# Products 512 columns wide in a two-layer decoder trunk: two token halves side by side, gate and up token-major with transposes back

## The chip, the core and the metric

The kernel runs on one core of one Trainium2 chip. Its engines work side by side, each through its own queue in order: TensorE (PE; its loading of the stationary operand is shown apart, as PEld), VectorE (DVE), ScalarE (ACT), GpSimd (POOL) and SyncE (SP, whose queue issues the DMAs). The metric is the time of one execution in microseconds (us), the median of several runs.

## What is computed

Two layers on 256 tokens (S) of 1024 features (D), float32. Layer 0 mixes tokens by causal attention (8 heads of 128; with 256 tokens there is one block, so the selection of past blocks adds nothing), layer 1 by a gated convolution of width 3. Each is followed by a SwiGLU feed-forward with D_FF = 2816. Scale, shift and gate of every sub-layer come from a vector c.

```python
for i in range(DEPTH):
    mod = sc @ w_ada[i] + b_ada[i]                       # sc = silu(c)
    sh_m, sc_m, g_m, sh_f, sc_f, g_f = jnp.split(mod, 6, axis=-1)
    h = modulate(x, norm_mix[i], sh_m, sc_m)
    y = moba_attention(h, ...) if i % 2 == 0 else short_conv(h, ...)   # both end in a product with 1024 x 1024 weights
    x = x + g_m[:, None, :] * y
    h = modulate(x, norm_ffn[i], sh_f, sc_f)
    g, u = jnp.split(h @ w_gate_up[i], 2, axis=-1)
    x = x + g_f[:, None, :] * ((jax.nn.silu(g) * u) @ w_down[i])
```

## The kernel before

**Products.** Every float32 operand is split into a high and a low float32r part, and every product is three PE instructions (`mm3`, L285): high by high, high by low, low by high. The one that is loaded has 128 columns, the one that moves has 256 (258 in the raw products below). A chunk of weights, up to 1024 rows by 256 columns, arrives by one DMA of 1 MB (`load`, L82, into one of five buffers `wf`); ACT casts it to the high part `wh` (L98), DVE subtracts to get the low part `wl` (L99), each in two halves.

**Feature-major.** The residual stream `xT` holds features on the partitions and the 256 tokens along the free axis. In `feat_gemm` and `out_proj` the weights are loaded and the 256 tokens move; the operands are pairs of separate tiles (high, low): `ov` and `zv` (input of the output projections of layers 0 and 1), `a0` and `a1` (input of the down-projections), `f0` and `f1` (normed input of gate and up).

**Feed-forward** (`ffn`, L466). Gate and up are done in 11 chunks `j` of 256 features each. The first goes by `raw_gemm` (L437), which multiplies the residual before its norm is known and corrects by the norm afterwards; the other ten fill `pg` and `pu`, then silu on ACT, `a = s * pu` on DVE (L481), and the split of `a` into the pair `av` (L434, L435). The down-projection `out_proj` (L406) goes through four groups of two output tiles, each with three chunks of 8, 8 and 6 blocks of 128 rows.

**The chain of a norm.** When an output tile of a projection is done, `residual` (L404, DVE) adds it to `xT` straight from the accumulator (PSUM), and `Norm.take` (L357) squares it (ACT), sums (POOL, L364, L367), and makes the raw pair: high part on ACT (L373), low part on DVE (L374). After the fifth tile the shift's columns are appended (L380, L381). The first raw product of the next stage reads these columns, so PE waits for L381; its third group of products waits for the sums (`ms`, L387), its fifth for the row of norms (`rr`, L335). The output projections `op_o` and `op_co` go through the groups [0, 1], [2], [3] of two tiles each; `op_d` is the down-projection.

**What sets the order.** The stream of chunks is a fixed list; between the weights stand 56 chunks of the modulation (`wa`), which DVE multiplies and adds up (L116). `get` prepares two chunks ahead of the one that PE takes up. Within these bounds a scheduler sets each engine's order before the run, and each engine keeps it.

**End.** The last down-projection's tiles are added to `xT`, turned to token-major by PE (L828), copied by ACT (L832) and stored by five DMAs (`store`, L825).

Of the kernel before, what the change touches and what calls it, by code (L numbers as in the profile page):

```python
# [31 lines left out]
def trunk_kernel(ctx: ExitStack, tc: tile.TileContext, x, c, w_ada, b_ada, norm_mix, norm_ffn, w_qkv, w_o,  # L32
# [69 lines left out]
    mod = const.tile([P, DEPTH * 48], F32, name="mod")  # L102
    acc_of = {}
    late, gets = [], [0]

    def ada_piece(l, part, i):
# [131 lines left out]

    def ffn_chunks(l):
        gu, dn = [], []  # L240
        for j in range(KF // 2):
            gu.append(w(("g", l, j), w_gate_up[l][:, j * CW:][:, :CW]))
            gu.append(w(("u", l, j), w_gate_up[l][:, D_FF + j * CW:][:, :CW]))
# [47 lines left out]
    def feat_gemm(parts, xs, nk):  # L291
        xh, xl = xs
# [7 lines left out]
    def tok_gemm(parts, xs, nk, between={}):  # L300
        xh, xl = xs
# [49 lines left out]
    class Norm:  # L351
        """Sums of squares over the features, gathered as the residual's tiles come."""
# [4 lines left out]
        def take(self, k):  # L357
# [13 lines left out]
            rh, rl = self.raw  # L371
# [30 lines left out]

# [463 lines left out]
```

## Time and profile before

| | |
|---|---|
| median of 3 runs | 625.7 us (625.13 to 626.88) |
| span of the profiled execution, first to last instruction | 622.1 us |
| the median less this span | 3.6 us |
| granted TensorE clock, mean | 0.999 |
| busy: PE, PEld, DVE, ACT, POOL | 98%, 96%, 76%, 52%, 3% |
| bytes over the DMA queues | 156.07 MB, mean 251 GB/s |

The page gives no other time of the profiled execution than its span. A row of the timeline gives start and duration in us, engine, line, operation, what is written and read, shape and count, and in brackets the idle time before it with what ended it. PE's durations overlap, since a product's end is still draining when the next one starts: the time that a product takes from PE is the distance of two starts, its pitch. A row of the stages' table gives from:to, length, then for PE, PEld, DVE, ACT and POOL the busy time with the number of instructions, the granted clock, the DMA engines' busy share, and GB/s. A row of the groups gives line, engine, operation, names, shapes, count, busy time and mean duration in ns, and the engine's idle time before these instructions with its causes.

### The profile page before, as it was taken

What the parts mean: (1) busy time and instruction counts of PE and PEld (TensorE: products, weight loads), DVE (VectorE), ACT (ScalarE), POOL (GpSimd) and SP (SyncE); (2) the same over time, 40 slices, a digit from 0 to 9 for tenths busy, and PEclk for the clock granted to TensorE, in tenths of its full rate; (3) what the DMA queues carried; (4) which work ended last, traced back from release to release, by engine and by line L of the source; (5) the groups of instructions that cost most, each with busy time, mean ns of one, the idle gap of its engine ahead of it and who ended that gap; (6) DMA issues with size and microseconds to landing.
All of it is one profiled execution on the core that took longest, in us unless ns stands there. A gap on an engine that the chain in (4) does not pass through costs nothing.

```text
span 622.1 us, 12512 instructions
## 1 busy us (share of the span) xinstructions
PE 609.7 (98%) x5291; PEld 595.8 (96%) x5291; DVE 473.6 (76%) x668; ACT 323.1 (52%) x518; POOL 19.2 (3%) x26
## 2 busy tenths in 40 slices
PE   7999999999999999999999999999999999999997
PEld 5789999999999999999999999998999999999997
DVE  5567999989989899979888989658976467644440
ACT  5335977466655455535355745545744435533330
POOL 0000000020000000000110000012000000000000
PEclk9999999999999999999999999999999999999999
DMA  9999999966699999798998497646388677655200
GB/s 271 329 331 354 385 370 335 303 219 223 210 323 322 347 333 335 257 318 303 319 302 278 133 304 241 210 138 205 108 299 271 201 225 235 204 188 178 94 18 17
DMA packets 127455, 156.07 MB, mean 251 GB/s; under 512 B 2822, under 2 KB 114856, under 8 KB 127400
## 3 DMA queue, kind: packets, MB, share of 16 engines
q1 hardware_dynamic: 127400, 155.28, 75.6%
q8 instruction: 41, 0.67, 0.5%
q14 instruction: 14, 0.11, 0.1%
HBM read 154.22 MB, written 1.05 MB: 250 GB/s over the span
## 4 chain that ended last, share of the span: by engine, by line
PE 88%; DMA 3%; DVE 3%; issue 3%; ACT 1%; SPq 0%; POOLq 0%; POOL 0%; ACTq 0%
PE pu L289 7%; PE pu L288 7%; PE op_d L287 7%; PE pu L287 7%; PE op_d L289 7%; PE op_d L288 7%; PE pg L289 6%; PE pg L288 6%; PE pg L287 6%; DMA wa<-in_w_ada_dram 2%; DMA wf_qk<-in_w_qkv_dram 1%; PE pv L287 1%; PE pb L288 1%; PE pv L289 1%; PE pb L287 1%
## 5 line engine op out<-in xcount | busy, mean ns | idle before, releaser
L116 DVE SCALAR_TENSOR_TENSOR acc<-wa,sc,acc 128x1024 f32<-128x1024 f32 x70 | 89.8, 1283 | 8.8 <-DMA wa<-in_w_ada_dram 7.5
L98 ACT ACTIVATE wh_d<-wf_d 128x1024 fp32r<-128x1024 f32 (+1 forms) x48 | 45.5, 981 | 69.7 <-issue 47.2
L99 DVE TENSOR_TENSOR wl_d<-wf_d,wh_d 128x1024 fp32r<-128x1024 f32 (+1 forms) x48 | 53.6, 1144 | 30.7 <-ACT wh_d L98 30.5
L98 ACT ACTIVATE wh_u<-wf_u 128x1024 fp32r<-128x1024 f32 x44 | 44.3, 1051 | 45.3 <-issue 34.5
L98 ACT ACTIVATE wh_g<-wf_g 128x1024 fp32r<-128x1024 f32 x44 | 45.5, 1050 | 40.7 <-issue 40.7
L99 DVE TENSOR_TENSOR wl_u<-wf_u,wh_u 128x1024 fp32r<-128x1024 f32 x44 | 52.7, 1233 | 14.0 <-ACT wh_u L98 14.0
L99 DVE TENSOR_TENSOR wl_g<-wf_g,wh_g 128x1024 fp32r<-128x1024 f32 x44 | 54.5, 1245 | 2.1 <-ACT wh_g L98 2.0
L287 PE MATMUL op_d<-a1h,wh_d 128*128 128x256 f32 x176 | 50.3, 286 | 0.0
L287 PE MATMUL op_d<-a0h,wh_d 128*128 128x256 f32 x176 | 50.2, 285 | 0.0
L289 PE MATMUL op_d<-a1h,wl_d 128*128 128x256 f32 x176 | 50.0, 284 | 0.0
L289 PE MATMUL op_d<-a0h,wl_d 128*128 128x256 f32 x176 | 50.0, 284 | 0.0
L288 PE MATMUL op_d<-a1l,wh_d 128*128 128x256 f32 x176 | 49.6, 282 | 0.0
L288 PE MATMUL op_d<-a0l,wh_d 128*128 128x256 f32 x176 | 49.5, 281 | 0.0
L289 PE MATMUL pg<-f1h,wl_g 128*128 128x256 f32 x160 | 44.8, 280 | 0.0
L289 PE MATMUL pu<-f1h,wl_u 128*128 128x256 f32 x160 | 44.8, 280 | 0.0
L287 PE MATMUL pg<-f1h,wh_g 128*128 128x256 f32 x160 | 44.6, 279 | 0.0
L288 PE MATMUL pg<-f1l,wh_g 128*128 128x256 f32 x160 | 44.6, 279 | 0.0
L287 PE MATMUL pu<-f1h,wh_u 128*128 128x256 f32 x160 | 44.6, 279 | 0.0
L288 PE MATMUL pu<-f1l,wh_u 128*128 128x256 f32 x160 | 44.6, 279 | 0.0
L287 PE MATMUL pg<-f0h,wh_g 128*128 128x256 f32 x160 | 44.5, 278 | 0.0
L289 PE MATMUL pg<-f0h,wl_g 128*128 128x256 f32 x160 | 44.4, 278 | 0.0
L289 PE MATMUL pu<-f0h,wl_u 128*128 128x256 f32 x160 | 44.4, 278 | 0.0
(315 smaller groups left out, 2103.6 us busy)
## 6 DMA issues: line engine op xcount, KB each, us to landing
wa<-in_w_ada_dram SPq DMA_DIRECT2D x40, 1024.0 KB, 6.1
wf_g<-in_w_gate_up_dram SPq DMA_DIRECT2D x22, 1024.0 KB, 6.6
wf_u<-in_w_gate_up_dram SPq DMA_DIRECT2D x22, 1024.0 KB, 7.5
wf_d<-in_w_down_dram SPq DMA_DIRECT2D x16, 1024.0 KB, 6.3
wa<-in_w_ada_dram SPq DMA_DIRECT2D x16, 512.0 KB, 7.1
wf_d<-in_w_down_dram SPq DMA_DIRECT2D x8, 768.0 KB, 5.7
wf_qk<-in_w_qkv_dram SPq DMA_DIRECT2D x8, 512.0 KB, 8.1
wf_v<-in_w_qkv_dram SPq DMA_DIRECT2D x4, 1024.0 KB, 7.5
```

The costliest lines, as they stand in the source:

```text
L98: nc.scalar.activation(wh[:, a:b], wf[:, a:b], AF.Copy)
L99: nc.vector.tensor_sub(wl[:, a:b], wf[:, a:b], wh[:, a:b].bitcast(F32))
L116: nc.vector.scalar_tensor_tensor(acc, w[:, kk], sc[:, k:k + 1], acc, op0=ALU.mult, op1=ALU.add)
L287: nc.tensor.matmul(ps, ah, bh, start=first, stop=False, skip_group_check=True)
L288: nc.tensor.matmul(ps, ah, bl, start=False, stop=False, skip_group_check=True)
L289: nc.tensor.matmul(ps, al, bh, start=False, stop=last, skip_group_check=True)
```

## The change

1. **Pairs in one tile.** High and low part of an activation lie in one tile (`[P, 2, nk, S]`), so that both can move in one instruction.
2. **`mm512` in `out_proj`.** For `op_o`, `op_co` and the down-projection of layer 0, the weights' high part is loaded once and the activations' high and low part move as 512 columns; then the low part of the weights with the high part of the activations, 256 columns. Two instructions stand where there were three. The accumulator has two halves, and `residual` adds one after the other: two DVE instructions for each tile instead of one.
3. **Gate and up token-major.** After the raw chunk come 5 blocks of 512 features instead of 10 of 256. The activations are loaded (128 tokens at a time) and 512 columns of weights move (`tok_wide`). A weight chunk is 512 rows by 512 columns, again 1 MB. Silu and product make `a` token-major, and `to_pair` turns it back: 8 PE transposes for each block, placed after the second k-step of the next gate block, and the split reads their PSUM tile.
4. **Last down-projection token-major** (`project`), 512 output features moving, in two halves of 6 chunks; `store` multiplies by the gate, adds the residual and stores, in four DMAs. The residual is turned to token-major earlier, between products of gate and up (`to_tokens`), the gate is made as a row on all partitions (`gate_rows`: two float32 products of 512 columns, and a DMA of the bias), and the sum over partitions in three bfloat16 parts goes for this one modulation.

Core of the diff (the pairs' indexing, comments and moved tiles left out):

```diff
+    def ps_wide(name):
+        return psum.tile([P, 2 * CW], F32, tag="gemm", name=name, bufs=4)
...
+        if (l, part) == (DEPTH - 1, G_F):
+            late.append((gets[0], lambda: gate_rows(acc)))
+            return
...
+    def gate_rows(acc):
+        for n in range(2):
+            cs = slice(n * 2 * CW, (n + 1) * 2 * CW)
+            ps = ps_misc(f"gate_ps_{n}")
+            nc.tensor.matmul(ps, one.to_broadcast([P, P]), acc[:, cs], start=True, stop=True)
+            nc.vector.tensor_add(last["gate"][:, cs], last["gate"][:, cs], ps)
...
+    WIDE = 2 * CW
+    GU_BLOCKS = (D_FF - CW) // WIDE
+    DOWN = ((0, 4), (4, 4), (8, 4), (12, 4), (16, 4), (20, 2))
...
+    def mm512(ps, lhs, both, first, last):
+        ah, al = lhs
+        nc.tensor.matmul(ps, ah, both, start=first, stop=False, skip_group_check=True)
+        nc.tensor.matmul(ps[:, 1], al, both[:, 0], start=False, stop=last, skip_group_check=True)
+
     def residual(ps, l, gate, k):
-        nc.vector.scalar_tensor_tensor(xT[:, k], ps, mcol(l, gate, k), xT[:, k], op0=ALU.mult, op1=ALU.add)
+        for n in range(2):
+            nc.vector.scalar_tensor_tensor(xT[:, k], ps[:, n], mcol(l, gate, k), xT[:, k], op0=ALU.mult, op1=ALU.add)
...
-                    mm3(pss[j, o], (wh[:, k, cs], wl[:, k, cs]), (xs[0][:, base + k], xs[1][:, base + k]),
-                        base + k == 0, base + k == total - 1)
+                    mm512(pss[j, o], (wh[:, k, cs], wl[:, k, cs]), xs[:, :, base + k],
+                          base + k == 0, base + k == total - 1)
...
+    def to_pair(pair, k, rows):
+        pt = ps_alt(f"ft_{k}")
+        for o in range(2):
+            for t in range(2):
+                nc.tensor.transpose(pt[:, o * S + t * P:][:, :P], rows[t][:, o * P:(o + 1) * P], ident)
+        split(pair, slice(k, k + 2), pt.rearrange("p (o s) -> p o s", s=S))
+
+    def tok_wide(pss, keys, xs, between={}, final=False):
+        total, base = sum(nk for _, nk in keys), 0
+        for i, (key, nk) in enumerate(keys):
+            wh, wl = get(key)
+            steps = [(k, t) for k in range(nk) for t in range(2)]
+            if final and i == len(keys) - 1:
+                steps.sort(key=lambda s: s[1])
...
+                mm3(pss[t], (xs[:, 0, base + k, ts], xs[:, 1, base + k, ts]), (wh[:, k], wl[:, k]),
+                    base + k == 0, base + k == total - 1)
+            base += nk
...
+    def store(j, t, cs, ps):
+        y = tmp.tile([P, WIDE], F32, tag="s", name=f"y_{j}_{t}")
+        nc.vector.tensor_mul(y, ps, last["gate"][:, cs])
+        nc.vector.tensor_add(y, y, last["x"][:, t, cs])
+        nc.sync.dma_start(of[:, t, cs], y)
```

**DVE, norm chain of the output projection of layer 1.** From the residual of the first tiles to the shift's columns, before (`op_co_j_o` is the accumulator of output tile o of group j, `a1` the pair that the raw products read, `wl_g_0` and `wl_u_0` the next weights):

```order
L404 SCALAR_TENSOR_TENSOR xT<-op_co_0_0_5029,mod,xT 128x256
L404 SCALAR_TENSOR_TENSOR xT<-op_co_0_1_5030,mod,xT 128x256
L404 SCALAR_TENSOR_TENSOR xT<-op_co_1_0_5031,mod,xT 128x256
L99 TENSOR_TENSOR wl_co_5070<-wf_co_5067,wh_co_5069 128x1024 x2
L374 SCALAR_TENSOR_TENSOR a1l<-xT,mod,a1h 128x256 x3
L404 SCALAR_TENSOR_TENSOR xT<-op_co_1_1_5032,mod,xT 128x256
L404 SCALAR_TENSOR_TENSOR xT<-op_co_2_0_5195,mod,xT 128x256
L99 TENSOR_TENSOR wl_g_0_5200<-wf_g_0_5197,wh_g_0_5199 128x1024 x2
L374 SCALAR_TENSOR_TENSOR a1l<-xT,mod,a1h 128x256 x2
L404 SCALAR_TENSOR_TENSOR xT<-op_co_2_1_5196,mod,xT 128x256
L99 TENSOR_TENSOR wl_u_0_5272<-wf_u_0_5269,wh_u_0_5271 128x1024
L381 TENSOR_TENSOR a1l<-mod,a1h 128x8x2
```

The last part of the same stretch with the change (L441 is the residual, L404 the low part of the raw pair, L411 the shift's columns), the first ten rows left out:

```order
L441 SCALAR_TENSOR_TENSOR xT<-op_co_1_1_4369,mod,xT 128x256
L103 TENSOR_TENSOR wl_g_0_4509<-wf_g_0_4506,wh_g_0_4508 128x1024
L404 SCALAR_TENSOR_TENSOR a_4365<-xT,mod,a_4365 128x256 x2
L103 TENSOR_TENSOR wl_g_0_4509<-wf_g_0_4506,wh_g_0_4508 128x1024
L441 SCALAR_TENSOR_TENSOR xT<-op_co_2_0_4504,mod,xT 128x256
L441 SCALAR_TENSOR_TENSOR xT<-op_co_2_1_4505,mod,xT 128x256
L441 SCALAR_TENSOR_TENSOR xT<-op_co_2_0_4504,mod,xT 128x256
L441 SCALAR_TENSOR_TENSOR xT<-op_co_2_1_4505,mod,xT 128x256
L103 TENSOR_TENSOR wl_u_0_4567<-wf_u_0_4564,wh_u_0_4566 128x1024
L404 SCALAR_TENSOR_TENSOR a_4365<-xT,mod,a_4365 128x256
L103 TENSOR_TENSOR wl_u_0_4567<-wf_u_0_4564,wh_u_0_4566 128x1024
L411 TENSOR_TENSOR a_4365<-mod,a_4365 128x8x2
```

Each tile's residual stands there twice: 12 residual rows lie ahead of L411 where 6 lay ahead of L381, with as many low parts (five) and weights, and the second half of `wl_u_0` has moved ahead of L411.

**DVE, the same chain in layer 0**, from the first half of `wl_u_0` to the first half of the next gate weights, before:

```order
L99 TENSOR_TENSOR wl_u_0_1815<-wf_u_0_1812,wh_u_0_1814 128x1024
L374 SCALAR_TENSOR_TENSOR a0l<-xT,mod,a0h 128x256
L99 TENSOR_TENSOR wl_u_0_1815<-wf_u_0_1812,wh_u_0_1814 128x1024
L381 TENSOR_TENSOR a0l<-mod,a0h 128x8x2
L404 SCALAR_TENSOR_TENSOR xT<-op_o_3_0_1810,mod,xT 128x256
L374 SCALAR_TENSOR_TENSOR a0l<-xT,mod,a0h 128x256
L404 SCALAR_TENSOR_TENSOR xT<-op_o_3_1_1811,mod,xT 128x256
L374 SCALAR_TENSOR_TENSOR a0l<-xT,mod,a0h 128x256
L99 TENSOR_TENSOR wl_g_1_1888<-wf_g_1_1885,wh_g_1_1887 128x1024
```

And with the change:

```order
L103 TENSOR_TENSOR wl_u_0_1768<-wf_u_0_1765,wh_u_0_1767 128x1024
L404 SCALAR_TENSOR_TENSOR a_1534<-xT,mod,a_1534 128x256
L441 SCALAR_TENSOR_TENSOR xT<-op_o_2_1_1695,mod,xT 128x256
L411 TENSOR_TENSOR a_1534<-mod,a_1534 128x8x2
L103 TENSOR_TENSOR wl_u_0_1768<-wf_u_0_1765,wh_u_0_1767 128x1024
L441 SCALAR_TENSOR_TENSOR xT<-op_o_3_0_1763,mod,xT 128x256
L404 SCALAR_TENSOR_TENSOR a_1534<-xT,mod,a_1534 128x256
L441 SCALAR_TENSOR_TENSOR xT<-op_o_3_0_1763,mod,xT 128x256
L441 SCALAR_TENSOR_TENSOR xT<-op_o_3_1_1764,mod,xT 128x256
L103 TENSOR_TENSOR wl_g_1_0_1826<-wf_g_1_0_1823,wh_g_1_0_1825 128x1024
L404 SCALAR_TENSOR_TENSOR a_1534<-xT,mod,a_1534 128x256
L441 SCALAR_TENSOR_TENSOR xT<-op_o_3_1_1764,mod,xT 128x256
```

Here the second half of `wl_u_0` moved behind L411, and between L411 and the last tile's last residual stand two halves of weights where before there was none.

**PE, second k-step of gate block 2 in layer 0.** Before, one k-step of a chunk of 256 features (`f0` moves, the weights are loaded, the right-hand name):

```order
L287 MATMUL pg_2_2183<-f0h,wh_g_2_2067 128x256
L288 MATMUL pg_2_2183<-f0l,wh_g_2_2067 128x256
L289 MATMUL pg_2_2183<-f0h,wl_g_2_2068 128x256
L287 MATMUL pg_2_2183<-f0h,wh_g_2_2067 128x256
L288 MATMUL pg_2_2183<-f0l,wh_g_2_2067 128x256
L289 MATMUL pg_2_2183<-f0h,wl_g_2_2068 128x256
```

With the change (512 columns of weights move, `f` is loaded), followed by the turning of the first four tiles of the block before:

```order
L314 MATMUL pg_2_0_2149<-wh_g_2_0_2079,f_1901 128x512
L315 MATMUL pg_2_0_2149<-wl_g_2_0_2080,f_1901 128x512
L316 MATMUL pg_2_0_2149<-wh_g_2_0_2079,f_1901 128x512
L314 MATMUL pg_2_1_2150<-wh_g_2_0_2079,f_1901 128x512
L315 MATMUL pg_2_1_2150<-wl_g_2_0_2080,f_1901 128x512
L316 MATMUL pg_2_1_2150<-wh_g_2_0_2079,f_1901 128x512
L508 MATMUL ft_2173<-ident,a_1_0_2145 128x128
L508 MATMUL ft_2173<-ident,a_1_1_2147 128x128
```

Six products of 512 columns stand for the work of twelve of 256, and 8 transposes (`ft`) come in, which wait for the two DVE products that write `a`.

More of the change, by code (lines that the diff above doesn't have):

```diff
@@ L103, in trunk_kernel @@
     acc_of = {}
-    late, gets = [], [0]
+    late, gets, last = [], [0], {}
     def ada_piece(l, part, i):
@@ L291, in feat_gemm @@
     def feat_gemm(parts, xs, nk):
-        xh, xl = xs
+        xh, xl = halves(xs)
         for k in range(nk):
@@ L370, in take @@
             self.n += 1
-            rh, rl = self.raw
+            rh, rl = halves(self.raw)
             a = mcol(self.l, self.scl, k)
@@ L421, in out_proj @@
                         last = k
-                        for fn, *args in between.get(k, ()):
+                        for fn, *args in between.get(base + k, ()):
                             fn(*args)
@@ L464, in raw_gemm, with project @@
         return res[0], res[1], hs
+    def to_pair(pair, k, rows):
[11 more added lines that the diff above has]
+                steps.sort(key=lambda s: s[1])
+            seen = set()
+            for k, t in steps:
+                if k not in seen:
+                    seen.add(k)
+                    for fn, *args in between.get(base + k, ()):
+                        fn(*args)
+                ts = slice(t * P, (t + 1) * P)
+                mm3(pss[t], (xs[:, 0, base + k, ts], xs[:, 1, base + k, ts]), (wh[:, k], wl[:, k]),
+                    base + k == 0, base + k == total - 1)
+            base += nk
+    def project(l, av, turns, done):
+        if l < DEPTH - 1:
+            out_proj([[(("d", l, j, i), n) for i, n in enumerate((8, 8, 6))] for j in range(4)], av, l, G_F, done,
+                     {2: turns})
+            return
+        for j in range(2):
+            cs = slice(j * WIDE, (j + 1) * WIDE)
+            pss = [ps_wide(f"y_{j}_{t}") for t in range(2)]
+            tok_wide(pss, [(("d", l, j, i), n) for i, (_, n) in enumerate(DOWN)], av, {2: turns} if j == 0 else {},
+                     final=True)
+            for t in range(2):
+                done(j, t, cs, pss[t])
     def ffn(l, norm, av, done):
-        for j in range(KF // 2):
+        turns = []
+        for j in range(1 + GU_BLOCKS):
             if j == 0:
@@ L822, in trunk_kernel, with to_tokens @@
     of = out[0].rearrange("(t p) d -> p t d", p=P)
-    o_sb = {}
-    def store(k):
-        ps = ps_misc(f"out_ps_{k}")
-        for t in range(2):
-            nc.tensor.transpose(ps[:, t * P:(t + 1) * P], xT[:, k, t * P:(t + 1) * P], ident)
-        j, o = divmod(k, 2)
-        if o == 0:
-            o_sb[j] = tmp.tile([P, 2, 2 * P], F32, tag="s", name=f"osb_{j}")
-        nc.scalar.activation(o_sb[j][:, :, o * P:(o + 1) * P], ps[:, :S].rearrange("p (t f) -> p t f", t=2), AF.Copy)
-        if j == 3:
-            nc.sync.dma_start(of[:, :, k * P:(k + 1) * P], o_sb[j][:, :, o * P:(o + 1) * P])
-        elif o == 1:
-            nc.sync.dma_start(of[:, :, j * 2 * P:(j + 1) * 2 * P], o_sb[j])
+    def store(j, t, cs, ps):
[3 more added lines that the diff above has]
+        nc.sync.dma_start(of[:, t, cs], y)
+    flat = act.tile([P, 3 * D], F32, tag="z", name="last_x")
+    last["x"] = flat[:, :2 * D].rearrange("p (t d) -> p t d", d=D)
+    last["gate"] = flat[:, 2 * D:]
+    nc.sync.dma_start(last["gate"], b_ada[DEPTH - 1:, G_F * D:].to_broadcast([P, D]))
+    def to_tokens(n):
+        pt = ps_misc(f"xt_{n}")
+        for o in range(2):
+            for t in range(2):
+                nc.tensor.transpose(pt[:, t * S + o * P:][:, :P], xT[:, 2 * n + o, t * P:(t + 1) * P], ident)
+        nc.scalar.activation(last["x"][:, :, n * S:(n + 1) * S], pt.rearrange("p (t f) -> p t f", t=2), AF.Copy)
+    last["turn"] = to_tokens
     ffn(1, n2, av, store)
```

105 lines of the change are left out of this document (61 added, 44 removed).

## The prediction, on record before the changed kernel was run

> **What bounds the kernel now.** I read the page first, then the table of stages, then the starts in the timeline.
>
> ```profile
> span 622.1 us, 12512 instructions
> ...
> PE 609.7 (98%) x5291; PEld 595.8 (96%) x5291; DVE 473.6 (76%) x668; ACT 323.1 (52%) x518; POOL 19.2 (3%) x26
> ```
>
> PE is the bound; the next engine is a fifth below it. The stages from the attention's output projection on:
>
> ```profile
> 112.40:140.00 27.60, 27.50 (x222) 25.98 (x220) 24.49 (x39) 15.98 (x31) 4.63 (x5) 1.00 0.80 257
> 140.00:154.10 14.10, 12.97 (x106) 12.77 (x107) 13.40 (x25) 9.06 (x17) 1.03 (x2) 1.00 0.70 243
> 154.10:266.66 112.56, 112.56 (x1034) 112.45 (x1033) 101.77 (x111) 61.32 (x75) 0.00 (x0) 1.00 0.89 302
> 266.66:331.40 64.74, 64.74 (x582) 64.65 (x580) 56.03 (x62) 31.46 (x44) 4.94 (x6) 1.00 0.92 306
> 401.27:424.40 23.13, 23.13 (x199) 23.13 (x195) 15.63 (x22) 12.13 (x21) 5.14 (x5) 1.00 0.50 160
> 424.40:438.87 14.47, 13.11 (x108) 12.69 (x107) 11.59 (x24) 7.85 (x16) 1.93 (x2) 1.00 0.55 182
> 438.87:552.55 113.68, 113.68 (x986) 113.64 (x985) 77.17 (x86) 56.94 (x70) 0.00 (x0) 1.00 0.68 222
> 552.55:617.65 65.10, 65.10 (x548) 64.82 (x544) 25.86 (x30) 20.10 (x27) 0.00 (x0) 1.00 0.29 95
> 617.65:622.10 4.45, 0.61 (x4) 0.20 (x2) 0.48 (x1) 0.77 (x2) 0.00 (x0) 0.84 0.21 59
> ```
>
> They are `op_o`, the raw products behind it (with the two raw chunks of gate and up), gate and up, the down-projection, then for layer 1 `op_co`, raw products, gate and up, down-projection, and the end. PE has no gap in the feed-forwards; only the two stretches of raw products show PE waiting, though DVE is nearly full there in the first. So a stage's time is the number of PE instructions by their pitch, except at the two norms.
>
> **Pitches.** Three places in the long stages, and at the attention and the last `op_d` the nearest rows to what the change adds:
>
> ```profile
> 500.00 0.28 PE L287 MATMUL pg<-f1h,wh_g 128*128 128x256 f32 x1
> ...
> 502.94 0.28 PE L288 MATMUL pu<-f1l,wh_u 128*128 128x256 f32 x1
> ...
> 299.84 0.28 PE L287 MATMUL op_d<-a0h,wh_d 128*128 128x256 f32 x1
> ...
> 302.96 0.28 PE L289 MATMUL op_d<-a0h,wl_d 128*128 128x256 f32 x1
> ...
> 96.21 0.60 PE L737 MATMUL po<-vp 128*128 128x256 f32 x2
> 96.65 0.38 PE L738 MATMUL po<-vp 128*128 128x128 f32 x2
> ...
> 108.97 0.59 PE L737 MATMUL po<-vp 128*128 128x256 f32 x2
> 109.40 0.38 PE L738 MATMUL po<-vp 128*128 128x128 f32 x2
> ...
> 110.32 0.49 PE L729 MATMUL prt<-ident,pr 128*128 128x128 f32 x3
> 110.65 0.39 PE L703 MATMUL s<-qkT 128*128 128x128 f32 x2
> ...
> 330.80 0.75 PE L151 MATMUL mod_ps<-one_b,part 128*128 128x1 bf16 x24
> 331.41 0.36 PE L287 MATMUL raw_m<-zvh,wh_cg 128*128 128x258 f32 x1
> ```
>
> In the first pair lie 25 products, in the second 26: (502.94 - 500.00)/25 = 0.1176 and 3.12/26 = 0.120 for 256 columns. No float32r product of 512 columns is in this trace. The nearest is `po`, plain float32: a product of 256 columns shows as two records, which take 0.44 and 0.43 together, 0.22 and 0.215 each; twice the stream of a float32r record, as 512 columns would be. The lower bound of the price is as far below as one likes only if a column gets cheaper with width, for which no row speaks; the upper one is two products of 256, 0.235. I take **0.2175**, the mean of the `po` rows: it says that a product has a fixed part of some 0.015 to 0.02, which the wide one pays once. A float32 transpose takes 0.33/3 = 0.11, a one-column product 0.61/24 = 0.025, with no gap to the next.
>
> **Feed-forwards.** Gate and up have 480 wide products where 960 stood: 480 x 0.2175 = 104.4. Layer 0 adds 32 transposes, 3.5, and keeps its 72 one-column products, 1.8: 109.7 for 112.56, **-2.9**. Layer 1 has 32 + 16 transposes (the residual's 16 come forward from the end), 5.3, and the two float32 products of the gate's row instead of 24 one-column ones, 1.7 (512 float32 columns, four times 0.215 each): 111.4 for 113.68, **-2.3**. The down-projection of layer 0 is 176 pairs of 0.2175 + 0.120 = 59.4, 8 transposes, 48 one-column products: 61.5 for 64.74, **-3.2**. The last one is 264 x 0.2175 = 57.4 and 8 transposes: 58.3 for 65.10, **-6.8**, the largest term, since all of its products stood at 0.120 and the residual's transposes have left it.
>
> The transposes wait for the two DVE products that write `a`. The products that stand ahead of them are their cover: two k-steps, 12 x 0.2175 = 2.6, against two of these:
>
> ```profile
> L116 DVE SCALAR_TENSOR_TENSOR acc<-wa,sc,acc 128x1024 f32<-128x1024 f32 x23 | 29.5, 1284 | 5.0 <-DMA wa<-in_w_ada_dram 4.6
> ...
> L481 DVE TENSOR_TENSOR a<-s,pu 128x512 f32<-128x512 f32 x10 | 6.8, 683 | 2.9 <-PE pu L289 2.9
> ```
>
> 2 x 0.68 = 1.4, so they fit, and with one other piece of 1.28 ahead in DVE's queue they just do. DVE waited 2.9 for `pu`: it was mostly there first. The row for the bias is one more DMA on SP's queue; it waits for `op_co` to end, and the weights queued behind it are two blocks ahead of PE: nothing. The end: four stores behind a product and a sum of 0.68 each against 4.45 before, which held transpose, copy and store: +0.3.
>
> **The two norms.** Here PE saves 64 x (3 x 0.120 - 0.2175 - 0.120) = 1.4 in each projection, 0.7 of it ahead of the first residual. But `residual` now runs twice for each tile on DVE, and the halves can't share a start. From before:
>
> ```profile
> 141.51 0.39 PE L288 MATMUL raw_f<-a0l,wh_g 128*128 128x258 f32 x1 [1.12 <-DVE a0l L381]
> ...
> 148.14 0.38 PE L335 MATMUL rr_n<-ident,rs_n 128*128 128x128 f32 x2
> ...
> 411.96 1.27 DVE L404 SCALAR_TENSOR_TENSOR xT<-op_co,mod,xT 128x256 f32<-128x256 f32 x3 [7.13 <-PE op_co L289]
> ...
> 424.96 0.39 PE L288 MATMUL raw_f<-a1l,wh_g 128*128 128x258 f32 x1 [0.32 <-DVE a1l L381]
> ...
> 428.99 0.38 PE L387 MATMUL ms_n<-inv_d,ss_n 128*128 128x1 f32 x2 [1.04 <-POOL ss_n L367]
> 432.87 0.38 PE L335 MATMUL rr_n<-ident,rs_n 128*128 128x128 f32 x2
> ...
> 426.36 0.86 DVE L404 SCALAR_TENSOR_TENSOR xT<-op_co,mod,xT 128x256 f32<-128x256 f32 x2
> ...
> 142.44 0.48 DVE L404 SCALAR_TENSOR_TENSOR xT<-op_o,mod,xT 128x256 f32<-128x256 f32 x1
> ...
> L99 DVE TENSOR_TENSOR wl_u<-wf_u,wh_u 128x1024 fp32r<-128x1024 f32 x44 | 52.7, 1233 | 14.0 <-ACT wh_u L98 14.0
> ```
>
> PE waits for DVE at L381 in both layers, and in layer 1 again for the sums that follow the last residual. A residual half costs 1.27/3 = 0.42, a half of the weights' low part 1.2. In layer 1 (order above) L411 gets 6 halves more and one half of `wl_u_0` ahead of it, and starts 0.7 earlier: 424.90 + 2.5 + 1.2 - 0.7 = 427.9, while the last residual, two more halves on, ended at 427.22 and comes to about 427.22 + 8 x 0.42 - 0.7 = 429.9. From the end of the last residual to `ms` it was 428.99 - 427.22 = 1.77, from there to `rr` 3.88; so `rr` stands at 435.5 for 432.87: **+2.6**. In layer 0 the second half of `wl_u_0` moves behind L411, so this one comes at about 141.47 + 2.5 - 1.2 - 0.7 = 142.1; but then six residual pieces (halves and low parts, which take as long) and two halves of weights (6 x 0.42 + 2.4 = 4.9) stand up to the end of the last residual, done at 147.0 for 142.92; 1.8 to `ms` and about 3.6 to `rr`: 152.3 for 148.14, **+4.2**. DVE was 13.40 of 14.10 busy there, so nothing absorbs it. Lower bound of both: the halves hide and PE's 1.4 stays, -1.4 each. I take the counted values, since the quoted waits for L381 show DVE late already in both layers. Behind the layer's `op_d` the chain had room (PE's raw products of the convolution run on); 0.
>
> **Sum.** -2.9 - 3.2 - 2.3 - 6.8 + 4.2 + 2.6 + 0.3 = -8.1. Span 622.1 - 8.1 = 614.0; the median lies 3.6 above the span: **617.6 us**. With the pitch between 0.215 and 0.22 for the 1528 wide products it is 613.8 to 621.4.
>
> **Rivals.**
> - *The norms don't pay* (0.14). The residual halves run in time that DVE spends waiting for PE, and both norms give -1.4: 6.8 + 2.8 = 9.6 less, 608.0. For it: 7.13 of idle before the first residual of `op_co`. Against: that idle lies before the chain, not in it.
> - *DVE becomes the bound in layer 0's feed-forward* (0.13). DVE is busy there 101.77 + 56.03 = 157.8 of 177.3; 8 more halves make 161.2. PE needs 109.7 + 61.5 = 171.2. If all 19.5 of DVE's idle time stayed, it would take 180.7, 9.5 too many; if only waits for the DMA and for ACT stayed (4.6 in the row above and the 3.4 in the row below), 169.2, which hides. Half way, 622.3.
>
> ```profile
> L99 DVE TENSOR_TENSOR wl_d<-wf_d,wh_d 128x1024 fp32r<-128x1024 f32 (+1 forms) x20 | 22.2, 1140 | 3.4 <-ACT wh_d L98 3.4
> ```
>
> - *A column has a price, an instruction has none* (0.09): slower. A product of 512 takes as long as two of 256, 0.235, and the transposes, the halves and the longer chains come on top: 1528 x 0.0175 = 26.7 more, **644.3**. It ends on the slow side from 0.2175 + 8.1/1528 = 0.2228 on. For it: the three 256-column streams are back to back, with nothing visible between them. Against: `po`, but it is float32 in several passes, not float32r.
> - *Transposes are dear* (0.03). If a transpose kept PE for its whole duration instead of overlapping with the next (three records last 0.49, of which two pitches are 0.22: 0.27 for one), 80 x 0.16 = 12.8 more: 630.4. Against: the starts, 0.11 apart, and the clock, which stays at 1.00 in the stages. The Trainium skill, "TensorE: Matmul & The Clock Gate", section "Part 4: PE-mode transpose", gives about 275 ns for a 128 x 128 transpose within a kernel and says that transposes don't keep the clock up; by that the sum would be 13.2 higher. The starts speak against it here.
> - *The width is free* (0.01). If a product of 512 took PE no longer than one of 256, 0.120, then 1528 x 0.0975 = 149 less, and DVE would bound: 473.6 + 24 x 0.42 + 3.6 = 487.3 at least. Against: both `po` rows. The Trainium skill, same page, section "Back-to-back issue gap", gives about 131 ns for each product of 512 columns in a stream and about 216 for an isolated one; by the first the sum would be 132 lower. The `po` rows, which stand in a stream, side with the second.
>
> **How the numbers follow.** The forecast has 0.60. A measurement of this kernel can tell about 0.3%, 1.9 us, from no change: faster means under 623.8, slower over 627.6. Forecast: 0.57 faster, 0.03 same; norms that don't pay: 0.14 faster; DVE bound: 0.08, 0.03, 0.02 slower; price by the column: 0.02 same, 0.07 slower; dear transposes 0.03 slower; free width 0.01 faster. Together 0.80, 0.08, 0.12. The range takes in the forecast with its pitches, the free norms at 608.0 with a pitch slightly lower (607.0), and the DVE case's middle with the pitch's upper bound (625.0); price by the column, dear transposes and free width, 0.13, are left out.
>
> **What would show it.** Right: `pg`, `pu` and `y` at a pitch of 0.215 to 0.22, the `op_d` pair at 0.3375, transposes at 0.11 with no idle time before them; last down-projection the largest gain (58.3); PE's wait before the shift's columns about 3 in layer 1 and a longer one before `ms` in both. Wrong: a pitch of 0.235 or a clock under 1; PE waiting for `a`, for weights or for DVE in layer 0's feed-forward; a chain of the norm that ends no later than before; PE idle before `gate_ps` (its modulation late) or a longer end.

## The result: 634.2 us, 1.014 of the time before

The changed kernel takes 634.17 us (median of 4 runs, 633.99 to 634.26), the kernel before, run beside it, 625.64: the ratio is 1.014 (95% interval 1.0124 to 1.0156), slower by 8.5 us, where 617.6 had been forecast. The profiled execution has a span of 632.3 us; before it was 622.1, so the profiles differ by 10.2 (the first lay 3.6 under the median of its kernel, this one 1.9). The profiled execution of the kernel before is one of its short ones (mean clock 0.999; many others have a span of 623.1 to 624.0 at 0.996 or 0.997), so 1.7 of the 10.2 are not the change's.

The first lines of the page with the change:

```profile
span 632.3 us, 9606 instructions
...
PE 616.8 (98%) x3823; PEld 534.0 (84%) x3823; DVE 482.4 (76%) x691; ACT 321.5 (51%) x512; POOL 21.1 (3%) x26
```

PE has 1468 instructions fewer and is busy 7 us longer. Its weight loads took 62 us less, and nothing shows for it: they had run beside the products. The stages, in the same columns as before (gate and up, down-projection, the two of layer 1, the end, then the two stretches with a norm):

```profile
156.16:273.36 117.20, 117.20 (x586) 95.10 (x585) 104.55 (x117) 62.25 (x77) 0.00 (x0) 1.00 0.85 295
273.36:337.27 63.91, 63.91 (x415) 55.73 (x411) 58.74 (x69) 31.59 (x43) 4.59 (x5) 1.00 0.86 288
447.98:566.27 118.29, 118.29 (x534) 95.92 (x533) 75.29 (x84) 57.70 (x72) 0.00 (x0) 1.00 0.64 214
566.27:627.64 61.37, 61.37 (x274) 50.35 (x272) 27.30 (x30) 18.36 (x21) 0.00 (x0) 1.00 0.29 94
627.64:632.30 4.66, 0.01 (x1) 0.00 (x0) 1.43 (x3) 0.00 (x0) 0.00 (x0) 0.71 0.30 113
407.56:432.71 25.15, 23.03 (x134) 19.51 (x132) 17.93 (x28) 13.23 (x23) 5.06 (x5) 1.00 0.51 156
432.71:447.98 15.27, 14.52 (x107) 14.31 (x107) 11.73 (x25) 6.92 (x15) 2.14 (x2) 0.89 0.57 192
113.42:141.98 28.56, 26.74 (x159) 22.48 (x157) 26.28 (x44) 15.86 (x31) 4.54 (x4) 1.00 0.74 245
141.98:156.16 14.18, 13.03 (x107) 12.82 (x108) 11.44 (x21) 7.86 (x15) 2.20 (x2) 1.00 0.74 249
```

| stage | before | with the change | difference | forecast |
|---|---|---|---|---|
| up to `op_o` | 112.40 | 113.42 | +1.0 | 0 |
| `op_o` and raw products | 41.70 | 42.74 | +1.0 | +4.2 |
| gate and up, layer 0 | 112.56 | 117.20 | +4.6 | -2.9 |
| down-projection, layer 0 | 64.74 | 63.91 | -0.8 | -3.2 |
| convolution | 69.87 | 70.29 | +0.4 | 0 |
| `op_co` and raw products | 37.60 | 40.42 | +2.8 | +2.6 |
| gate and up, layer 1 | 113.68 | 118.29 | +4.6 | -2.3 |
| last down-projection and end | 69.55 | 66.03 | -3.5 | -6.5 |
| sum | | | +10.2 | -8.1 |

PE is without a gap in gate and up, as before: no wait for `a`, for weights or for DVE. What is dearer are the products. Their starts, and eight turns (the transposes `ft`) between two of them:

```profile
184.91 0.40 PE L314 MATMUL pg<-wh_g,f 128*128 128x512 f32 x1
...
189.79 0.40 PE L314 MATMUL pg<-wh_g,f 128*128 128x512 f32 x1
...
595.75 0.39 PE L315 MATMUL y<-wl_d,a 128*128 128x512 f32 x1
...
599.83 0.39 PE L315 MATMUL y<-wl_d,a 128*128 128x512 f32 x1
...
181.25 1.03 PE L508 MATMUL ft<-ident,a 128*128 128x128 f32 x8
182.04 0.48 PE L314 MATMUL pg<-wh_g,f 128*128 128x512 f32 x1
182.36 0.39 PE L315 MATMUL pg<-wl_g,f 128*128 128x512 f32 x1
```

From 184.91 to 189.79 lie 21 products: 0.232 each. From 595.75 to 599.83 lie 18: 0.227. Eight turns take 0.79, and the product behind them 0.32 where the others take 0.23: 0.88 together, 0.11 for each turn, as forecast.

### The profile page after: what moved, and what is told of

It reads as the page before. It is cut to its first block, busy times and chain, and to the rows that moved or that the text cites. A ratio compares the mean times of both kernels' runs of the same rounds, so it can differ in the third digit from the quotient of the medians.

```text
span 632.3 us, 9606 instructions
## 1 busy us (share of the span) xinstructions
PE 616.8 (98%) x3823; PEld 534.0 (84%) x3823; DVE 482.4 (76%) x691; ACT 321.5 (51%) x512; POOL 21.1 (3%) x26
## 4 chain that ended last, share of the span: by engine, by line
PE 88%; DVE 5%; DMA 3%; issue 2%; ACT 1%; SPq 0%; POOL 0%; POOLq 0%; ACTq 0%
PE pu L314 7%; PE pu L315 7%; PE pu L316 7%; PE op_d L436 7%; PE pg L314 6%; PE pg L316 6%; PE pg L315 6%; PE op_d L437 3%; PE y L316 3%; PE y L315 3%; PE y L314 3%; DMA wa<-in_w_ada_dram 2%; DMA wf_qk<-in_w_qkv_dram 1%; PE ft L508 1%; PE pv L314 1%
## 5 line engine op out<-in xcount | busy, mean ns | idle before, releaser
L102 ACT ACTIVATE wh_d<-wf_d 128x1024 fp32r<-128x1024 f32 (+2 forms) x48 | 44.8, 981 | 64.7 <-PE y L316 27.7
L103 DVE TENSOR_TENSOR wl_d<-wf_d,wh_d 128x1024 fp32r<-128x1024 f32 (+2 forms) x48 | 53.7, 1154 | 30.8 <-ACT wh_d L102 30.7
L314 PE MATMUL pg<-wh_g,f 128*128 128x512 f32 x160 | 64.0, 400 | 0.0
L314 PE MATMUL pu<-wh_u,f 128*128 128x512 f32 x160 | 63.2, 395 | 0.0
L316 PE MATMUL pg<-wh_g,f 128*128 128x512 f32 x160 | 63.2, 395 | 0.0
L315 PE MATMUL pu<-wl_u,f 128*128 128x512 f32 x160 | 63.2, 395 | 0.0
L316 PE MATMUL pu<-wh_u,f 128*128 128x512 f32 x160 | 63.1, 395 | 0.0
L315 PE MATMUL pg<-wl_g,f 128*128 128x512 f32 x160 | 63.1, 394 | 0.0
L436 PE MATMUL op_d<-a,wh_d 128*128 128x512 f32 x176 | 62.0, 398 | 0.0
L437 PE MATMUL op_d<-a,wl_d 128*128 128x256 f32 x176 | 49.1, 279 | 0.0
L316 PEld LDWEIGHTS pu<-wh_u,f 128*128 128x128 f32 x160 | 30.1, 188 | 7.1
L314 PEld LDWEIGHTS pu<-wh_u,f 128*128 128x128 f32 x160 | 30.1, 188 | 7.1
L316 PEld LDWEIGHTS pg<-wh_g,f 128*128 128x128 f32 x160 | 30.1, 188 | 7.1
L314 PEld LDWEIGHTS pg<-wh_g,f 128*128 128x128 f32 x160 | 30.1, 188 | 6.6
```

The lines of the kernel that those rows point to most:

```text
L102: nc.scalar.activation(wh[:, a:b], wf[:, a:b], AF.Copy)
L103: nc.vector.tensor_sub(wl[:, a:b], wf[:, a:b], wh[:, a:b].bitcast(F32))
L314: nc.tensor.matmul(ps, ah, bh, start=first, stop=False, skip_group_check=True)
L315: nc.tensor.matmul(ps, ah, bl, start=False, stop=False, skip_group_check=True)
L316: nc.tensor.matmul(ps, al, bh, start=False, stop=last, skip_group_check=True)
L436: nc.tensor.matmul(ps, ah, both, start=first, stop=False, skip_group_check=True)
```

## The experiments

Two theories stood against each other. A: a wide product costs what its columns cost, the turns come on top. B: the wide product is cheap in itself, and something that the change brings with it (transposes in the stream, the doubled residual, operands in other tiles) makes it dear. Ratios are to the kernel before, run beside each kernel; differences of stages come from the profiles.

**No turns.**

```diff
-        pt = ps_alt(f"ft_{k}")
-        for o in range(2):
-            for t in range(2):
-                nc.tensor.transpose(pt[:, o * S + t * P:][:, :P], rows[t][:, o * P:(o + 1) * P], ident)
-        split(pair, slice(k, k + 2), pt.rearrange("p (o s) -> p o s", s=S))
+        for t in range(2):
+            split(pair, k + t, rows[t])
```

> The changed kernel without its 80 transposes: the split reads the token-major tiles as they are, so the down-projections get a wrongly laid out operand, and all else stays. Theory A (a wide product costs what its columns cost, 0.231 to 0.237 for 512 in gate and up, and the transposes come on top at 0.109 each): 80 x 0.109 = 8.7 less, 625.5, the pitch in gate and up stays at 0.232 to 0.234. Theory B (a wide product costs 0.227, as in the last down-projection, and the transposes throw the stream of gate and up into a dearer rhythm): another 960 x 0.0065 = 6.2 less, 619.2.

Measured: 629.78 us, ratio 1.0102 (1.0083 to 1.0121). Gate and up of both layers and the down-projections behind them:

```profile
155.75:269.46 113.71, 113.71 (x555) 91.82 (x553) 104.98 (x125) 62.72 (x85) 0.00 (x0) 1.00 0.85 292
269.46:332.47 63.01, 63.01 (x406) 54.82 (x403) 56.66 (x67) 32.12 (x45) 5.68 (x5) 1.00 0.88 297
446.71:561.33 114.62, 114.62 (x502) 92.60 (x501) 75.50 (x92) 58.54 (x80) 0.00 (x0) 1.00 0.65 221
561.33:621.76 60.43, 60.43 (x266) 49.53 (x264) 27.35 (x32) 18.51 (x23) 0.00 (x0) 1.00 0.28 95
```

The four stages lose 3.5, 0.9, 3.7 and 0.9: 9.0 for 80 turns, and no more. Without any turn, gate and up of layer 0 still takes 113.71 where the 256-column products took 112.56. So the turns don't disturb the stream, and the part of B that blames them falls. What the place of the operands does, this run can't tell. The convolution's stage lost 3.4 here (73.73 for 70.29), for a reason of its own that is told at the end.

**Narrow.** The same layout with products of 256 columns:

```diff
-                mm3(pss[t], (xs[:, 0, base + k, ts], xs[:, 1, base + k, ts]), (wh[:, k], wl[:, k]),
-                    base + k == 0, base + k == total - 1)
+                for n in range(2):
+                    cs = slice(n * CW, (n + 1) * CW)
+                    mm3(pss[t][:, cs], (xs[:, 0, base + k, ts], xs[:, 1, base + k, ts]), (wh[:, k, cs], wl[:, k, cs]),
+                        base + k == 0 and n == 0, base + k == total - 1)
```

> The changed kernel with each token-major product of 512 columns as two of 256 (weights reloaded for the second), order of all else kept: 2448 narrow products for 1224. Theory A (price by the column): two narrow ones at 0.1133 to 0.120 each take 277 to 294 against 960 x 0.2335 + 264 x 0.2275 = 284 now, with 0.1178 as before 288: between 7 less and 10 more, most likely 4 more, 638. The theory of the forecast (each instruction has a fixed part of about 0.0155 beside its columns): 1224 x 0.0155 = 19 more, 653.

Measured: 643.33 us, ratio 1.0303 (1.029 to 1.0316), 9.2 more than the changed kernel by the spans. Of these 1.25 are raw products of layer 1 (16.52 for 15.27), which differ as much between two profiles of one program (`after_again` below).

```profile
155.97:275.41 119.44, 119.44 (x1067) 119.31 (x1065) 104.36 (x117) 62.25 (x77) 0.00 (x0) 1.00 0.82 285
451.33:572.03 120.70, 120.70 (x1014) 119.98 (x1013) 75.28 (x84) 57.70 (x72) 0.00 (x0) 1.00 0.62 211
572.03:636.80 64.77, 64.77 (x538) 64.33 (x536) 27.38 (x30) 18.33 (x21) 0.00 (x0) 1.00 0.26 88
```

Width is worth 2.24 and 2.41 in gate and up, 0.005 for each wide product, and 3.40 in the last down-projection, 0.013. Together that is 8.1, near the upper end of A and less than half of what the forecast's fixed part asks for (19). The width does save a little against two narrow products of the same layout. In gate and up the kernel before had cheaper narrow ones (0.113 to 0.118 for 0.119 here); in the last down-projection both have 0.120.

**Without the 512-column pair** in the output projections and in the down-projection of layer 0:

```diff
-                    mm512(pss[j, o], (wh[:, k, cs], wl[:, k, cs]), xs[:, :, base + k], ...)
+                    mm3(pss[j, o], (wh[:, k, cs], wl[:, k, cs]), (xs[:, 0, base + k], xs[:, 1, base + k]), ...)
```

with one residual instead of two on an accumulator of 256 columns.

> The changed kernel with three products of 256 and one residual in the output projections and the down-projection of layer 0 (pairs in one tile, gate and up and the last down-projection as changed). If the doubled residual costs at the norms what the traces differ by (1.0 in layer 0, 2.8 in layer 1) and the pair of products saves 0.0085 a time in the down-projection (176 x 0.0085 = 1.5 lost here): 2.3 less, 631.9, and the clock does not fall in the raw products of layer 1. If the halves are not the cause of the norms' loss: 304 x 0.0085 = 2.6 more, 636.8.

```profile
114.25:141.86 27.61, 27.45 (x223) 25.93 (x221) 24.49 (x39) 15.98 (x31) 4.62 (x5) 1.00 0.77 255
141.86:156.01 14.15, 13.03 (x107) 12.83 (x107) 13.36 (x25) 9.06 (x17) 1.03 (x2) 1.00 0.70 248
273.27:338.86 65.59, 65.59 (x591) 65.50 (x587) 56.09 (x63) 32.07 (x45) 4.86 (x6) 1.00 0.87 289
409.13:431.85 22.72, 22.72 (x198) 22.72 (x195) 15.36 (x21) 12.12 (x21) 4.88 (x5) 1.00 0.50 153
431.85:446.55 14.70, 13.19 (x109) 12.78 (x107) 11.81 (x24) 7.83 (x16) 2.17 (x2) 1.00 0.65 230
```

By stages as expected: the norm of layer 0 is 1.0 shorter than with the change (41.76), that of layer 1 3.0 (37.42, and the clock stays at 1.00), the down-projection 1.7 longer. The time, 632.91 us, ratio 1.0133 (1.0118 to 1.0148), can't be told from the changed kernel's: 0.8 of the gain was lost again ahead of `op_o`, where this edit changes nothing. That part stays open.

**The doubled residual alone**, in the kernel before (the second adds zero times the accumulator):

```diff
-        nc.vector.scalar_tensor_tensor(xT[:, k], ps, mcol(l, gate, k), xT[:, k], op0=ALU.mult, op1=ALU.add)
+        for col in (mcol(l, gate, k), zero_col):
+            nc.vector.scalar_tensor_tensor(xT[:, k], ps, col, xT[:, k], op0=ALU.mult, op1=ALU.add)
```

> The kernel before with each residual followed by a second one that adds zero times the accumulator: DVE gets the doubled residual, PE nothing of the change. If the doubling is what the norms lose: 2.8 more at the output projection of layer 1, 1.0 to 4 more in layer 0, nothing behind the down-projection: 629.5 to 632.5. If DVE takes the halves in its idle time: no more than 1.9 from 625.6.

Measured: 630.69 us, ratio 1.0098 (1.0084 to 1.0111).

```profile
111.33:140.68 29.35, 27.85 (x223) 25.97 (x221) 26.23 (x44) 15.86 (x31) 4.53 (x4) 1.00 0.72 242
140.68:154.65 13.97, 13.05 (x107) 12.84 (x108) 13.05 (x26) 7.98 (x15) 2.20 (x2) 1.00 0.72 248
154.65:270.08 115.43, 115.36 (x1034) 115.02 (x1033) 103.45 (x112) 62.16 (x78) 0.00 (x0) 1.00 0.87 297
404.68:429.92 25.24, 23.53 (x198) 22.91 (x194) 17.90 (x28) 12.28 (x22) 5.04 (x5) 1.00 0.48 157
429.92:445.22 15.30, 14.55 (x107) 14.34 (x107) 11.80 (x26) 7.71 (x16) 2.14 (x2) 0.89 0.46 154
```

The norms lose 1.6 (43.32 for 41.70) and 2.9 (40.54 for 37.60): the halves on DVE are what the two norms pay, and DVE doesn't take them in idle time. But gate and up of layer 0 also lost 2.9, where DVE had room and PE hardly waited. In the kernel before its narrow products start 0.1178 apart at first, and from 199.97 on, behind 24 one-column products of the modulation, 0.1133:

```profile
214.00 0.28 PE L287 MATMUL pg<-f0h,wh_g 128*128 128x256 f32 x1
...
217.06 0.28 PE L287 MATMUL pu<-f0h,wh_u 128*128 128x256 f32 x1
```

(27 products in 3.06.) With the zero column they stay at 0.1178 throughout. No instruction of this stage is new; every tile behind the column stands 32 bytes further in its partition, and the stage's instructions come at other moments. Which of the two keeps the pitch up is not shown. So within one stage, with its tiles in one place, the pitch can have two values.

**Only the last down-projection**, and that with the pair in the down-projection of layer 0; gate and up feature-major, three products of 256 columns in the output projections, pairs in one tile:

```diff
-            tok_wide(pg, [(("g", l, j, i), 4) for i in range(2)], hs, {2: turns})
...
+            feat_gemm([(pg, get(("g", l, j)))], hs, KD, {2: [(last["turn"], j - 1)]} if l == DEPTH - 1 and j < 5 else {})
+            feat_gemm([(pu, get(("u", l, j)))], hs, KD)
```

> Of the change only the pairs in one tile and the last down-projection token-major (with the gate's rows and the residual's 16 transposes between products of gate and up); gate and up feature-major in 256 columns, three products and one residual in the other projections. By theory A with the traces' stages: the last down-projection 264 x 0.2267 + 0.3 = 60.2 for 66.2, -6.0; in gate and up 16 x 0.11 + 1.3 for the gate's rows - 0.6 for the one-column products, +2.5; the end +1.3; the pairs' dearer rhythm in start, attention and convolution +1.4. Sum -0.8: 0.999 of the kernel before. If the cheap pitch of the last products (0.227) comes from the transposes ahead of them and the products go at 0.237 to 0.240 here, 3.5 more: 1.004.

> As last_only, and in the down-projection of layer 0 the pair of 512 and 256 columns with the doubled residual. Pair at 0.2355 + 0.116 for 3 x 0.120: 176 x 0.0085 = 1.5 less than last_only, 0.996 of the kernel before, if DVE hides the halves behind that projection. Rival: the halves lengthen the norm's chain there as they do at the output projections, by 2 or more, and it is no faster than last_only.

> The changed kernel once more, on the chip of the two others: 1.014 of the kernel before, and the same stages as in its first profile within 0.5 each, if the rhythm of the products (0.232 in gate and up, 0.227 in the last down-projection) belongs to the program. If the rhythm is an accident of one execution, stages of gate and up differ by 960 x 0.005 = 2 to 5.

Measured: 1.005 (1.0033 to 1.0068), 1.0024 (1.0011 to 1.0037), and 1.0149 (1.0128 to 1.0169) for the changed kernel once more. Its stages came out within 0.2 of the first profile, but for the raw products of layer 1 (16.54 for 15.27, where the clock fell later; see the end), so these pitches belong to the program. In `last_only` the last down-projection goes at 0.227 without any turn ahead of it, against the second reading in its expectation:

```profile
155.00:270.93 115.93, 115.93 (x1035) 115.81 (x1033) 102.17 (x111) 60.92 (x75) 0.00 (x0) 1.00 0.88 298
...
560.30:620.75 60.45, 60.45 (x266) 49.54 (x264) 26.70 (x29) 17.72 (x20) 0.00 (x0) 1.00 0.28 94
```

Yet it is slower than before, since gate and up of layer 0, with the same instructions, takes 115.93 for 112.56. `last_opd` brings 1.7 in its down-projection (63.01 for 64.72), and nothing of the convolution's norm is lost: there the halves hide.

**Where the operands stand.** Three tries. First the two parts of the features in two tiles instead of one (`Two` holds both and is indexed like one tile):

```diff
-        return act.tile([P, 2, nk, S], F32R, tag=tag, name=name)
+        return Two(*(act.tile([P, nk, S], F32R, tag=tag + p, name=name + p) for p in "hl"))
```

in the changed kernel for the normed inputs alone (`f_apart`), in `last_only` for all pairs (`last_apart`), in `last_opd` for all but the down-projections' inputs (`last_apart_opd`).

> The changed kernel with high and low part of the normed inputs of the projections of features (f0, f1 and the attention's and convolution's) in two tiles instead of one; nothing reads these as one, and no instruction is added or removed. If lying in one tile is what makes the rhythm of the stream dearer: narrow products in the convolution back at 0.1178 from 0.1187 (0.4 less), the start about 1 less, wide products of gate and up towards 0.227 (960 x 0.005 = 4.8 less): up to 6 less, 1.005. If it is not the tile: 1.014 as before.

> As last_only, but all pairs in two tiles as in the kernel before: only the last down-projection goes token-major. Against last_only, if the tile sets the rhythm: 3.4 less in gate and up of layer 0, 0.85 less in layer 1, 0.4 in the convolution, 0.9 in the start: 5.5 less, that is 1.9 less than the kernel before, 0.997. If the rhythm belongs to the order of instructions: as last_only, 1.005.

> As last_apart, with the down-projections' inputs in one tile and the pair of 512 and 256 columns in the down-projection of layer 0, as in last_opd. 1.7 less than last_apart, 0.994, if the inputs of the down-projections have no part in the rhythm of gate and up; about 1 more than that if the start's loss comes from the one tile that holds q, k, v there.

`f_apart`: 1.0148 (1.013 to 1.0165), every stage as with the change. The two tiles had landed where the one had been, side by side, so this told only that one tile or two doesn't matter. `last_apart`: 0.9989 (0.9976 to 1.0003); gate and up of layer 0 is back at 112.54, but the last products now go at 0.233 and their stage takes 62.15. `last_apart_opd`: 621.62 us, ratio 0.9938 (0.9923 to 0.9954), 0.6% under the kernel before, with an interval that leaves out 1:

```profile
154.18:266.72 112.54, 112.54 (x1035) 112.43 (x1033) 101.87 (x111) 61.22 (x75) 0.00 (x0) 1.00 0.89 303
266.72:329.73 63.01, 63.01 (x407) 54.83 (x403) 57.66 (x66) 31.20 (x42) 4.71 (x5) 1.00 0.87 296
...
554.80:615.21 60.41, 60.41 (x266) 49.54 (x264) 26.69 (x29) 17.73 (x20) 0.00 (x0) 1.00 0.27 94
```

The ratio is the one expected, but in part by luck: beside the 1.7 of the down-projection, two things that nobody expected nearly cancel. The last products went back to 0.227 (1.7 less than in `last_apart`), and the raw products of layer 1 took 1.5 more (15.97 for 14.50), with the clock halved for a while.

Then the place alone, in the changed kernel: the tile of the normed inputs is set up ahead of another one, and no instruction changes; with the gap of 64 bytes (the first added line, in `f_first_gap` alone) it starts elsewhere again.

```diff
+    act.tile([P, 16], F32, name="gap")
+    act.tile([P, 2, KD, S], F32R, tag="h", name="h_place")
     x_flat = act.tile([P, 4 * D], F32, tag="z", name="x_tok")
```

> The changed kernel, the same instructions in the same order, but the tile of the normed inputs (f) stands 24,704 bytes lower in each partition: its start, taken modulo 2048, goes from 96 to 2016, the place that the weights and the activations of the down-projections have. If the places of a product's operands set the rhythm: gate and up go at 0.227 as the last down-projection, 960 x 0.006 = 5.8 less, and the convolution changes its 0.1187; 1.005. If the place has no part in it: 1.014 and the same stages within 0.3.

> As f_first, with a gap of 64 bytes ahead of that tile, so that it starts at 32 modulo 2048, as in the kernel before; the tile of the convolution's output moves with it. If the place sets the rhythm: narrow products of the convolution at 0.1178 as before (0.4 less than 70.30 for its stage), wide products of gate and up at another pitch than 0.232 to 0.237, up to 5 less in all. If not: 1.014.

Measured: 630.92 us, 1.0101 (1.0085 to 1.0116), and 633.11 us, 1.0142 (1.0125 to 1.0159). Gate and up, convolution, gate and up of `f_first`:

```profile
156.69:271.26 114.57, 114.57 (x586) 94.87 (x585) 104.09 (x117) 62.24 (x77) 0.00 (x0) 1.00 0.88 303
335.16:406.08 70.92, 70.92 (x616) 70.88 (x613) 61.34 (x93) 40.21 (x58) 0.74 (x1) 1.00 0.72 238
447.74:563.36 115.62, 115.62 (x534) 95.71 (x533) 75.22 (x84) 57.70 (x72) 0.00 (x0) 1.00 0.65 219
```

and of `f_first_gap`:

```profile
155.02:272.56 117.54, 117.54 (x586) 94.63 (x585) 104.36 (x117) 62.23 (x77) 0.00 (x0) 1.00 0.85 294
336.47:406.31 69.84, 69.84 (x617) 69.80 (x613) 60.88 (x91) 39.98 (x58) 1.51 (x1) 1.00 0.72 237
446.62:565.18 118.56, 118.56 (x535) 95.67 (x533) 75.28 (x84) 57.67 (x72) 0.00 (x0) 1.00 0.63 214
```

With the same instructions in the same order on PE, 64 bytes move each gate and up by 3.0, and the convolution by 1.1 the other way. Of the tiles that PE reads in gate and up only the normed inputs moved. That the place of an operand has a part in the pitch is shown; by which rule is not. In these runs the wide products with activations loaded took 0.227 where the activations' tile starts, like the weights, at 2016 modulo 2048 (`f_first`; the last down-projections except that of `last_apart`), and 0.232 to 0.233 where it, or its high part, starts at 32 or 96.

Neither expectation came out whole. In `f_first` gate and up got 5.3 of the 5.8 expected, but the start lost 0.5, the convolution 0.6 and the raw products of layer 1 1.2, so the ratio is 1.010 and not 1.005. In `f_first_gap` the convolution is back where the kernel before had it (69.84 for 69.87), but the wide products got no cheaper. So each theory has a part: turns on top of a price by the column, at best 0.2267 for 512 (A), and up to 0.007 more for each wide product by the place, some 3 in each gate and up (B).

## Why the prediction was wrong, by its steps

- **The pitch of a wide product** is the step that failed: "I take 0.2175, the mean of the `po` rows: it says that a product has a fixed part of some 0.015 to 0.02, which the wide one pays once." From the stages, less turns (0.11), one-column products (1.8) and the gate's row (1.3): gate and up (117.20 - 1.8 - 3.5)/480 = 0.233, in layer 1 (118.29 - 1.3 - 5.3)/480 = 0.233; the pair in `op_d` (63.91 - 0.9 - 1.2)/176 = 0.351 for 0.3375; the last products (61.37 - 0.9 - 0.4)/264 = 0.2275. The four misses, 480 x 0.0156 + 480 x 0.0152 + 176 x 0.0138 + 264 x 0.010, make 19.9, more than the 18.3 between forecast and profile. The `po` rows are of another kind of product, and the trace had a better row than these: narrow products at 0.1133, from 199.97 on. Twice that is 0.2267, the best pitch that a wide product reached in any run: nothing is left over for a fixed part of 0.015. Against narrow products of the same layout (`narrow`) the width saved 0.005 or 0.013, by the stage.
- So the rival of the price by the column had the mechanism nearly right. Its size was too high: it put all wide products at 0.235 (644.3), and by stages they took 0.2275 to 0.235.
- **Turns**: 80 at 0.11 and hidden waits, as forecast: 9.0 measured. The prediction was right here, and the gain that was to pay for them wasn't there: 3.5 of the 4.6 that gate and up of layer 0 lost are turns, the rest is 480 wide products at 0.233 for 960 narrow ones at 0.115.
- **The norm of layer 1**: +2.6 forecast, +2.8 measured, by the chain named. PE waits for it in two pieces, first 1.49 for ACT's high part of the shift's columns (L410), which the prediction didn't name, then 0.75 for L411. The first product behind L411 starts 26.6 behind the start of `op_co` (before 23.7), `rr` 34.5 (31.6):

```profile
432.71 0.51 PE L314 MATMUL raw_f<-a,wh_g 128*128 128x258 f32 x2 [1.49 <-ACT a L410]
...
434.21 0.39 PE L315 MATMUL raw_f<-a,wh_g 128*128 128x258 f32 x1 [0.75 <-DVE a L411]
...
442.04 0.27 PE L365 MATMUL rr_n<-ident,rs_n 128*128 128x128 f32 x1
```

  The clock fell behind these waits, a sign of being wrong that the prediction named and didn't count. In this profile it cost nothing that shows, since `ms` came 1.9 behind the last residual (forecast 1.8); in `after_again` it fell later, and the raw products took 1.3 longer. That the size came out so near is in part luck.
- **The norm of layer 0**: +4.2 forecast, +1.0 measured. The chain was late as forecast, `rr` 39.7 behind the start of `op_o` for 35.7. But I took it that as many raw products follow `rr` as before. They don't:

```profile
146.91 0.38 PE L417 MATMUL ms_n<-inv_d,ss_n 128*128 128x1 f32 x2 [1.15 <-POOL ss_n L397]
...
153.08 0.38 PE L365 MATMUL rr_n<-ident,rs_n 128*128 128x128 f32 x2
...
156.16 0.40 PE L314 MATMUL pg<-wh_g,f 128*128 128x512 f32 x1
```

  Gate and up starts 3.1 behind `rr`, before it was 6.0: the order has 24 raw products behind it instead of 48, and PE did the others in time that I had counted as waiting. The order of PE's instructions was there to be read before the run; I had read DVE's alone.
- **The end**: +0.3 forecast, +0.2 measured: the last store now starts behind two DVE instructions of 0.69, and from PE's end it takes 4.66 for 4.45.
- **DVE as the bound in layer 0** didn't come: PE's busy time fills the stage.
- The start and the convolution (+1.4), not in the forecast, have the same products in the same order. Both follow the place of the tiles: 70.92 and 69.84 for the convolution in `f_first` and `f_first_gap`, 113.95 and 112.23 for the start.

## What to carry to other kernels

Before counting on fewer, wider matrix products, find the cheapest narrow product of the same data type in the trace: its pitch times two is a price by the column, and width saved no more here than what the narrow products at hand took above that price, 0 to 0.013 a product against 0.11 for each transpose that the new layout needs. The down-projections, which need no turning back, did gain: with them alone (`last_apart_opd`) the time is 0.994 of the kernel before. Where an edit lets a late chain end later, look at what the changed order leaves behind it on the waiting engine before adding the delay to the end. And when two versions are compared, see whether untouched stages keep their pitch: here the place of one operand's tile moved the two stages of gate and up by 5.9 us, where the edit lost 9.2 and the turns alone took 7.2.

## What the runs showed of the hardware

The pitch of a back-to-back float32r product takes one of a few values: 0.1133, 0.1178, 0.119 or 0.120 for 256 columns, 0.227 or 0.232 to 0.237 for 512. Another profile of the changed kernel showed the same ones within 0.001. A pitch stays until something else comes between, and can be another one behind it: in gate and up of the kernel before 0.1178 and then 0.1133, in the down-projection of layer 0 with the change 0.347 and then 0.353 for a pair, both times behind one-column products. Placing an operand 64 bytes further on changes it too, and what is good for wide products (`f_first`: 0.227 in gate and up) is bad for narrow ones (0.120 in its convolution).

The granted clock can fall behind a short wait of PE. With the change the two waits of 1.49 and 0.75 shown above lie close together, and then the granted clock halves:

```profile
433.00:436.00 3.00, 2.25 (x15) 2.04 (x15) 3.00 (x7) 1.69 (x4) 0.01 (x1) 0.84 0.78 255
436.00:438.00 2.00, 2.00 (x11) 2.00 (x11) 1.26 (x2) 1.03 (x3) 1.85 (x1) 0.50 0.91 346
```

In the run without turns it fell behind one wait at the convolution's norm. DVE, which had pieces of the modulation and of the weights first, began the residuals 1.3 behind the end of the down-projection's stage there; with the turns it began them 1.2 ahead of it.

```profile
337.26 0.38 PE L417 MATMUL ms_n<-inv_d,ss_n 128*128 128x1 f32 x2 [1.67 <-POOL ss_n L397]
```

```profile
338.00:342.00 4.00, 4.00 (x22) 4.00 (x23) 1.18 (x2) 0.26 (x1) 0.00 (x0) 0.57 0.89 302
```

In layer 0 the wait of 1.15 shown above, 3.8 behind one of 1.09, left it at 1.00. The length of a wait doesn't decide alone: in `last_apart_opd` the clock fell behind a single wait of 1.00, and in `last_apart` and in the kernel before it stayed at 1.00 behind 1.02 and 1.04 at the same place. Nor is the moment fixed: in `after_again` it fell only behind a third wait of 0.98, when the first two had been 1.48 and 0.76. First `last_apart_opd`, then `after_again`:

```profile
428.50:432.00 3.50, 3.50 (x19) 3.50 (x19) 0.65 (x2) 0.17 (x1) 0.00 (x0) 0.52 0.90 310
```

```profile
439.50:443.00 3.50, 3.50 (x20) 3.50 (x19) 1.72 (x3) 0.00 (x0) 0.00 (x0) 0.55 0.23 30
```

What sets the moment and the occasion is not shown. The Trainium skill, "TensorE: Matmul & The Clock Gate", section "What's actually happening", ties the half clock to an idle window of about 3.4 us; here it followed waits of half that length and less (1.67, 1.00).
